# Up projection of a conv-FFN: eight of its 22 column groups computed with tokens on partitions, in chunks of which every second takes seven block products

## The chip, the cores and the metric

The kernel runs on one core of one Trainium2 chip. The time is the device time of one execution in microseconds, here the median of three runs.

## The reference

Two layers on an input of 256 tokens by 2048 features, all in float32. Each layer has a token mixer (a spatial-gating MLP in the first, a latent attention in the second), and then the feed-forward part that this change is about. Cut to that:

```python
D_MODEL, SEQ, D_FF, CONV_W = 2048, 256, 5504, 3

def conv_ffn(x, w_up, conv_w, conv_b, w_down):
    h = x @ w_up                                    # 2048 -> 11008
    h = lax.conv_general_dilated(h, conv_w[:, None, :], window_strides=(1,),
                                 padding=[(CONV_W - 1, 0)], ...,
                                 feature_group_count=C) + conv_b   # causal, per channel
    a, g = jnp.split(h, 2, axis=-1)
    return (jax.nn.silu(g) * a) @ w_down            # 5504 -> 2048

for i in range(2):
    m = gmlp_mixer(x, ...) if i == 0 else mla_mixer(x, ...)
    x = layer_norm(ALPHA * x + m, ...)
    x = layer_norm(ALPHA * x + conv_ffn(x, ...), ...)
```

## The kernel before

**Precision.** Each product of float32 matrices is made of three products of a shorter type: a number is split into a high part and the remainder, and the kernel adds high·high, low·high and high·low. Weights come as chunks of 1 MB (128 partitions by 2048). The class `Feed` loads them (`raw`, three rooms, SyncE's queue), casts the high part `wh` on ScalarE (L125) and subtracts to get the low part `wl` on VectorE (L128). Split chunks live in 14 rooms called "big"; six more are called "side". PSUM has eight banks of 512 columns. Temporaries are in two rings, `t1` (6) and `t2` (5).

**Sevens.** A product of 2×2 blocks needs eight block products; with sums of blocks it needs seven (the Strassen–Winograd form). The kernel uses this for pairs of k: `Feed._seven` makes four sums `ts` of the chunk's blocks on VectorE (L135) and splits both `raw` and `ts`, into `wh`, `wl`, `th`, `tl`; `Banks.seven` issues 21 products of 512 columns, `Banks.eight` 24. A `seven` needs four more banks (`p1`, `q5`, `p7`, `p6`, called OWN) besides the four DIRECT ones (`q3`, `p2`, `e`, `q4`), sums of activation blocks (`combine`), and at the end of a group `rest`, which makes the four corrections from the OWN banks. The first mixer's input projections, its output projection and the down projections work so already. In the first of these, the v projection, a group has eight chunks in the order 0, 2, 1, 3, 5, 4, 6, 7, with sevens at 2, 3, 4 and 6.

**Parked sevens.** Eight chunks of each down projection are prepared during the up projection: `Feed.park` loads one over GpSimd's queue (`praw`), splits it (`pwh`, `pwl`), adds its blocks, splits the sums (`pth`, `ptl`), and stores all four in DRAM; `Feed.fetch` brings them back (`fwh`, `fwl`, `fth`, `ftl`). A unit is four steps of an iterator, advanced by `next(jobs, None)`. Unit 266 is the last parked of the first layer; 231 and 236 are the first two that the down projection uses. These tiles take "side" rooms.

**The up projection** has 86 chunks per layer in 22 groups (four chunks each, the last two). A group is 256 channels of `a` and the same of `g`. Group 0 is computed with tokens on partitions beside the norm of the mixer (`boundary`). Groups 1 to 21 have weights stationary (`prod_a`): per chunk 16 products of 512 columns with `wh`, which multiply high and low parts of the activations at once, and 16 of 256 with `wl`. Their result has channels on partitions, as the convolution along tokens wants it. `sum_halves` adds the two halves (`lo_`, `h_`), `conv` makes bias and three taps (`c_`), `pair` the gate. In groups 2 to 5 the norm's other parts are loaded back and finished (`restore`, `park` of the class `Norm`, on `res` and `lnp`). The first three activations for the down projection are made in groups 19 and 20 (`acts.make`, `dn00wx` and others).

The program's scheduler fixes each engine's order when the kernel is built, under the dependencies and with the rooms available; an instruction then waits on its engine's queue for semaphores, and all behind it wait too.

## Time and profile before

| | |
|---|---|
| median of three runs | 2465.41 us (2465.39 to 2465.87) |
| profiled execution: span | 2464.6 us, and its clock at 1.000 |
| TensorE (PE) busy | 2458.1 us, 100% |
| VectorE (DVE) busy | 2054.7 us, 83% |
| ScalarE (ACT) busy | 1459.3 us, 59% |
| up projection, TensorE, products with `wh`, `wl` | 611.4 us, 328.1 us busy (2624 each) |

The profile is of one execution, on one core, whose span is 0.8 us below the median. A row of the timeline gives start, length, engine, line, operation and, in square brackets, how long the engine had been idle before it and what ended that. A row of a window gives the busy time of PE, PEld (weight load), DVE, ACT and POOL (GpSimd), with the count of instructions, then the clock granted to TensorE, the DMA engines' busy share and GB/s. Lengths overlap where an engine starts the next instruction before the last has drained, so the distance between two starts may be shorter than the first one's length. The chain of waits is the chain of work that ended last.

### The profile page before, as it was taken

What the parts mean: (1) busy time and instruction counts of PE and PEld (TensorE: products, weight loads), DVE (VectorE), ACT (ScalarE), POOL (GpSimd) and SP (SyncE); (2) the same over time, 40 slices, a digit from 0 to 9 for tenths busy, and PEclk for the clock granted to TensorE, in tenths of its full rate; (3) what the DMA queues carried; (4) which work ended last, traced back from release to release, by engine and by line L of the source; (5) the groups of instructions that cost most, each with busy time, mean ns of one, the idle gap of its engine ahead of it and who ended that gap; (6) DMA issues with size and microseconds to landing.
All of it is one profiled execution on the core that took longest, in us unless ns stands there. A gap on an engine that the chain in (4) does not pass through costs nothing. (4 is left out here: it accounts for less than half of the span.)

```text
span 2464.6 us, 32483 instructions
## 1 busy us (share of the span) xinstructions
PE 2458.1 (100%) x12494; PEld 2091.3 (85%) x12494; DVE 2054.7 (83%) x2734; ACT 1459.3 (59%) x1967; POOL 104.2 (4%) x202
## 2 busy tenths in 40 slices
PE   9999999999999999999999999999999999999999
PEld 7888888888888888888888888988888888888887
DVE  7999999989897788778777997867598787878798
ACT  6666665566565666656554566665565665555453
POOL 0000000000000000000001000000000000000000
PEclk9999999999999999999999999999999999999999
DMA  7555666656665778778868885544478787777885
GB/s 291 202 208 205 226 204 202 205 188 205 222 212 198 241 282 314 300 279 300 322 218 318 301 301 182 184 170 156 172 269 309 275 305 304 295 265 278 299 324 201
DMA packets 116428, 611.94 MB, mean 248 GB/s; under 512 B 10648, under 2 KB 10912, under 8 KB 75184
## 3 DMA queue, kind: packets, MB, share of 16 engines
q1 hardware_dynamic: 90128, 462.47, 52.9%
q0 software_dynamic: 26144, 147.39, 15.8%
q8 instruction: 98, 1.61, 0.3%
q14 instruction: 58, 0.48, 0.1%
HBM read 544.75 MB, written 65.06 MB: 247 GB/s over the span
## 5 line engine op out<-in xcount | busy, mean ns | idle before, releaser
L128 DVE TENSOR_TENSOR wl<-raw,wh 128x1024 fp32r<-128x1024 f32 (+4 forms) x645 | 958.4, 1501 | 169.5 <-ACT wh L125 124.0
L125 ACT CAST wh<-raw 128x1024 fp32r<-128x1024 f32 (+4 forms) x645 | 809.0, 1278 | 356.8 <-PE up L230 80.7
L230 PE MATMUL up<-xhl,wh 128*128 128x512 f32 x2624 | 611.4, 390 | 0.0
L230 PEld LDWEIGHTS up<-xhl,wh 128*128 128x128 f32 x2624 | 487.4, 188 | 97.8
L230 PEld LDWEIGHTS up<-xhl,wl 128*128 128x128 f32 x2624 | 325.8, 192 | 6.4
L230 PE MATMUL up<-xhl,wl 128*128 128x256 f32 x2624 | 328.1, 283 | 0.0
L125 ACT CAST th<-ts 128x1536 fp32r<-128x1536 f32 (+1 forms) x138 | 142.5, 1052 | 110.9 <-DVE ts L135 80.3
L230 PE MATMUL ub<-wh,xhl 128*128 128x512 f32 x576 | 179.5, 393 | 0.0
L128 DVE TENSOR_TENSOR tl<-ts,th 128x1536 fp32r<-128x1536 f32 (+1 forms) x138 | 163.2, 1221 | 10.4 <-PE dn_p L230 3.4
L230 PEld LDWEIGHTS ub<-wh,xhl 128*128 128x128 f32 x576 | 108.1, 188 | 24.2 <-issue 1.9
L230 PE MATMUL ub<-wl,xhl 128*128 128x512 f32 x288 | 112.1, 389 | 0.0
L135 DVE TENSOR_TENSOR ts<-ts,raw 128x512 f32<-128x512 f32 x138 | 95.1, 689 | 1.4
L135 DVE TENSOR_TENSOR ts<-raw 128x1024 f32<-128x1024 f32 x69 | 84.3, 1221 | 6.1 <-PE ub L230 3.8
L230 PE MATMUL mo<-wh,oT 128*128 128x512 f32 x256 | 82.5, 401 | 0.0
L230 PE MATMUL v_q<-wh,xhl 128*128 128x512 f32 x224 | 70.7, 391 | 0.3 <-ACT wh L125 0.3
L230 PEld LDWEIGHTS ub<-wl,xhl 128*128 128x128 f32 x288 | 54.1, 188 | 11.3
L230 PE MATMUL v_p<-wh,xhl 128*128 128x512 f32 x192 | 59.9, 389 | 0.0
L230 PEld LDWEIGHTS mo<-wh,oT 128*128 128x128 f32 x256 | 45.5, 189 | 7.1
L230 PEld LDWEIGHTS v_q<-wh,xhl 128*128 128x128 f32 x224 | 42.0, 188 | 10.5 <-ACT wh L125 1.9
L230 PE MATMUL mo<-wl,oT 128*128 128x512 f32 x128 | 50.1, 391 | 0.0
L724 ACT ACTIVATE lny<-lnt,lncol 128x128 f32<-128x128 f32 x96 | 36.6, 472 | 15.6 <-PE lnt L720 15.5
L388 DVE TENSOR_TENSOR h_0a<-up,lo_0a 128x256 f32<-128x256 f32 x41 | 17.2, 421 | 33.0 <-ACT lo_0a L386 33.0
(1838 smaller groups left out, 4338.4 us busy)
## 6 DMA issues: line engine op xcount, KB each, us to landing
raw<-in_ffn_up_dram SPq DMA_DIRECT2D x172, 1024.0 KB, 7.0
raw<-in_gm_in_dram SPq DMA_DIRECT2D x93, 1024.0 KB, 5.3
raw<-in_ffn_dn_dram SPq DMA_DIRECT2D x68, 1024.0 KB, 7.2
raw<-in_gm_wout_dram SPq DMA_DIRECT2D x48, 1024.0 KB, 5.3
praw<-in_ffn_dn_dram POOLq DMA_DIRECT2D x16, 1024.0 KB, 13.9
keptth<-pth POOLq DMA_DIRECT2D x16, 1024.0 KB, 8.1
kepttl<-ptl POOLq DMA_DIRECT2D x16, 1024.0 KB, 8.8
fth<-keptth POOLq DMA_DIRECT2D x16, 1024.0 KB, 9.4
```

The lines of the kernel that those rows point to most:

```text
L125: cast = self.nc.scalar.copy(hi, raw)
L128: self.nc.vector.tensor_tensor(lo, raw, hi.bitcast(F32), ALU.subtract)
L135: add = lambda o, a, b: self.nc.vector.tensor_tensor(o, a, b, ALU.add)
L230: recent[0] = nc.tensor.matmul(o, l, r, start=start, stop=stop, skip_group_check=True)
L388: nc.vector.tensor_tensor(h, acc[:, 0:S], lo, ALU.add)
L724: nc.scalar.activation(y[:, j], t[:, j * P : (j + 1) * P], AF.Identity, bias=lncol[:, o : o + 1], scale=lncol[:, g : g + 1])
```

## The change

Per layer, groups 5 and 6 together, and 8 and 9 together, become one *token group* each: eight chunks with tokens on partitions, each chunk 256 k by 1024 columns, in the v projection's order and with sevens at the same four places. A token group has all eight banks. `sum_acts` makes the four activation sums that sevens need, two in group 2 and two in group 4, in two "side" rooms. After the last chunk `rest` and four more sums give the group's four results in SBUF; in the next group (7 and 10), behind its first chunk, 16 transposes (`turn_group`) bring them to channels on partitions, in four banks `upr`, and behind its second and third chunk the convolutions and gates follow (`gate_group`), reading those banks without `sum_halves`. Parked work leaves groups 5, 6, 8 and 9: its steps now stand in groups 2 to 4, at the end of 7 and 10, and in groups 11 to 20, three in odd and two in even ones. All four norm restores move to groups 1 and 2, the norm's parking to 2 and 3. Line numbers grow: L125, L128, L135 and L230 become L129, L132, L139 and L234.

```diff
--- before.py
+++ after.py
@@ -52,6 +52,10 @@
 U_PAIRS = [[0, 1, 5, 7, 2, 6, 3, 4]] + [[0, 1, 2, 5, 3, 7, 4, 6]] * 5
 U_SEVEN = [(2, 3)] + [(2, 3, 4)] * 4 + [(2, 3)]
 
+UP_TOKEN = (5, 8)
+UP_PAIRS = (0, 2, 1, 3, 5, 4, 6, 7)
+UP_SEVEN = (2, 3, 4, 6)
+
 T1, T2 = 6, 5
 SLOTS = {"big": 14, "raw": 3, "side": 6}
 
@@ -264,14 +268,27 @@
                     parked.append(len(chunks))
                 chunks.append((w[2 * u : 2 * u + 2, :, c].rearrange("k p c -> p k c"), 2048, kind))
 
+    def up(layer):
+
+        for gi in range(22):
+            if gi - 1 in UP_TOKEN:
+                continue
+            if gi not in UP_TOKEN:
+                chunks.extend((ffn_up[layer, i], 2048, "") for i in range(4 * gi, min(4 * gi + 4, n_up)))
+                continue
+            for p in UP_PAIRS:
+                i = 4 * gi + p // 2
+                w = ffn_up[layer, i : i + 5 : 4, :, p % 2 * 1024 : p % 2 * 1024 + 1024].rearrange("f p c -> p f c")
+                chunks.append((w, 2048, "seven" if p in UP_SEVEN else "wide"))
+
     back(gm_wout, NF_GM)
-    chunks += [(ffn_up[0, i], 2048, "") for i in range(n_up)]
+    up(0)
     back(ffn_dn[0], NF_FF)
     chunks += [(ml_q[i], 2048, "") for i in range(4)]
     chunks += [(ml_kv[i], 3 * KVR, "") for i in range(5)] + [(ml_kv[5, :, 0:KVR], KVR, "")]
     chunks += [(ml_b[i], 2048, "") for i in range(ml_b.shape[0])]
     chunks += [(ml_out[i], 2048, "") for i in range(ml_out.shape[0])]
-    chunks += [(ffn_up[1, i], 2048, "") for i in range(n_up)]
+    up(1)
     back(ffn_dn[1], NF_FF)
 
 
@@ -940,26 +957,83 @@
         boundary(ln, acc, end, f"upf{layer}_", after)
         xhl, old = ln.new, ln
         jobs = park_all(feed.used + 2 * n_up)
+        sums, rooms, turning = {}, [], []
+
+        def sum_acts(p):
+
+            if len(sums) % 2 == 0:
+                rooms.append(slot([P, 2, 8 * P], f"xs{layer}_{p}", F32R, "side" if len(rooms) < 2 else "big"))
+            t = xhl[p // 2][:, 2 * (p % 2) : 2 * (p % 2) + 2]
+            raw = tp.tile([P, 2, S], F32, tag="t2", name=f"xr{layer}_{p}", bufs=T2)
+            nc.vector.tensor_tensor(raw, t[:, :, 0:S].bitcast(F32), t[:, :, S : 2 * S].bitcast(F32), ALU.add)
+            sums[p] = combine(f"{layer}_{p}", rooms[-1][:, len(sums) % 2, :], raw[:, 0], raw[:, 1])
+
+        def token_group(gi):
+
+            acc = Banks(f"upt{layer}_{gi}", DIRECT + OWN)
+            for c, p in enumerate(UP_PAIRS):
+                a = [[x_parts(xhl, 2 * p + j, b) for j in range(2)] for b in range(2)]
+                got = feed.next()
+                if p in UP_SEVEN:
+                    acc.seven(a, sums[p], *got, turned=512, across=True)
+                    if p == [q for q in UP_PAIRS if q in UP_SEVEN][-1]:
+                        rest = acc.rest()
+                else:
+                    acc.eight(a, *got, across=True)
+            for n, t in zip(DIRECT, rest):
+                nc.vector.tensor_tensor(t, acc.acc[n], t, ALU.add)
+            turning.append((gi, rest, [bank(f"upr{layer}_{gi}_{i}") for i in range(4)]))
+
+        def turn_group():
+
+            gi, rest, t = turning[0]
+            for i, r in enumerate(rest):
+                b, f = i // 2, i % 2
+                for j in range(4):
+                    o = (j % 2) * S + b * P
+                    nc.tensor.transpose(t[2 * f + j // 2][:, o : o + P], r[:, j * P : (j + 1) * P], ident)
+
+        def gate_group(f):
+
+            gi, rest, t = turning[0]
+            for j in range(2):
+                c = slice(j * S, (j + 1) * S)
+                pair(2 * (gi + f) + j, t[2 * f][:, c], t[2 * f + 1][:, c])
+            if f == 1:
+                turning.pop()
+
         for gi in range(1, 22):
+            if gi - 1 in UP_TOKEN:
+                continue
+            if gi in UP_TOKEN:
+                token_group(gi)
+                continue
             nt, nk = (4, 4) if gi < 21 else (2, 8)
             acc = [bank(f"up{layer}_{gi}_{f}") for f in range(nt)]
             for c in range(KD // nk):
                 hi, lo = feed.next()
                 prod_a(acc, xhl, range(nk * c, nk * c + nk), hi, lo)
-                if gi > 1 and c in (1, 2) and gi + c > 3:
+                if gi > 1 and c in ((1, 2, 3) if gi > 10 and gi % 2 or gi - 2 in UP_TOKEN else (1, 2)) and gi + c > 3 and not turning:
                     next(jobs, None)
                 if (gi, c) in FIRST:
                     acts.make(*plan(NF_FF)[0][FIRST.index((gi, c))])
+                if turning and c == 0:
+                    turn_group()
+                if turning and c in (1, 2):
+                    gate_group(c - 1)
+                if gi in (2, 4) and c < 2 and len(sums) < len(UP_SEVEN):
+                    sum_acts(UP_SEVEN[len(sums)])
                 if gi == 1 and c == 0:
                     after(1, 1, None)
                     for f in range(2):
                         pair(f, hb[0][:, f * S : (f + 1) * S], hb[1][:, f * S : (f + 1) * S])
             for f in range(nt // 2):
                 pair(2 * gi + f, acc[f], acc[nt // 2 + f])
-            if 1 < gi < 6:
-                old.restore(gi - 2)
-            if gi in (4, 6):
-                old.park(gi // 2 - 2)
+            if gi < 3:
+                old.restore(2 * gi - 2)
+                old.restore(2 * gi - 1)
+            if gi in (2, 3):
+                old.park(gi - 2)
         ln = Norm(2 * layer + 1, {}, old.put_away, last)
         return (ln, *down(NF_FF, act, f"dn{layer}", ln, acts, 4 if last else SKEW))
```

Three places of the new order. Names are those of the tiles with their buffer numbers; a chunk's number stands in `wh178` and the like; layer 0 is shown.

TensorE, second token group, in what were groups 8 and 9. Before, the start of group 8, where chunks 176 and 177 follow one another in plain products (the first products with `wh176`, and with `wl177`):

```order
L230 MATMUL up0_8_0_7592<-xhl1_0_5782,wh176_7470 128x512 [waits Activation_49]
L230 MATMUL up0_8_1_7593<-xhl1_0_5782,wh176_7470 128x512 [waits DVE_49,PE_49]
L230 MATMUL up0_8_2_7594<-xhl1_0_5782,wh176_7470 128x512 [waits DVE_49]
L230 MATMUL up0_8_3_7595<-xhl1_0_5782,wh176_7470 128x512 [waits DVE_49,PE_49]
L230 MATMUL up0_8_0_7592<-xhl1_1_5783,wl177_7515 128x256 [waits DVE_49]
L230 MATMUL up0_8_1_7593<-xhl1_1_5783,wl177_7515 128x256
```

Now the same weights' place, chunks 177 and 178:

```order
L234 MATMUL upt0_8_e_7562<-wh178_7568,xhl1_0_5782 128x512 x2
L234 MATMUL upt0_8_e_7562<-wl178_7569,xhl1_0_5782 128x512
L234 MATMUL upt0_8_q4_7563<-wh178_7568,xhl1_0_5782 128x512 x2
L234 MATMUL upt0_8_p7_7566<-th177_7469,xs0_2_6345 128x512 [waits DVE_49]
L234 MATMUL upt0_8_p7_7566<-th177_7469,xs0_2_6345 128x512
L234 MATMUL upt0_8_p7_7566<-tl177_7470,xs0_2_6345 128x512
L234 MATMUL upt0_8_q4_7563<-wl178_7569,xhl1_0_5782 128x512
L234 MATMUL upt0_8_q4_7563<-wh178_7568,xhl1_0_5782 128x512 x2
L234 MATMUL upt0_8_q4_7563<-wl178_7569,xhl1_0_5782 128x512
L234 MATMUL upt0_8_p6_7567<-th177_7469,xs0_2_6345 128x512 [waits DVE_49,PE_49]
```

The products `p7` and `p6` of chunk 177 stand inside chunk 178, and wait for VectorE.

VectorE at the end of group 7. Before, half-sums, convolutions and the gate of group 7's last pair and group 8's first, with the split of chunk 181:

```order
L388 TENSOR_TENSOR h_0g15_7583<-up0_7_3_7381,lo_0g15_7581 128x256 [waits Activation_49]
L910 SCALAR_TENSOR_TENSOR c_0a15_7577<-h_0a15_7575,cst_176,c_0a15_7577 128x254 [waits DVE_49]
L128 TENSOR_TENSOR wl181_7727<-raw181_7642,wh181_7726 128x1024 [waits Activation_49]
L908 SCALAR_TENSOR_TENSOR c_0g15_7585<-h_0g15_7583,cst_176,c_0g15_7585 128x255 [waits Activation_49]
L910 SCALAR_TENSOR_TENSOR c_0g15_7585<-h_0g15_7583,cst_176,c_0g15_7585 128x254 [waits DVE_49]
L925 TENSOR_TENSOR act0_1_6893<-s0_15_7589,c_0a15_7577 128x256 [waits Activation_49]
L388 TENSOR_TENSOR h_0a16_7769<-up0_8_0_7592,lo_0a16_7767 128x256 [waits Activation_49]
L908 SCALAR_TENSOR_TENSOR c_0a16_7771<-h_0a16_7769,cst_176,c_0a16_7771 128x255 [waits Activation_49]
L388 TENSOR_TENSOR h_0g16_7777<-up0_8_2_7594,lo_0g16_7775 128x256 [waits Activation_49]
L910 SCALAR_TENSOR_TENSOR c_0a16_7771<-h_0a16_7769,cst_176,c_0a16_7771 128x254 [waits DVE_49]
L908 SCALAR_TENSOR_TENSOR c_0g16_7779<-h_0g16_7777,cst_176,c_0g16_7779 128x255 [waits Activation_49]
```

Now, the same pair (15) between the sums and splits of chunk 179:

```order
L132 TENSOR_TENSOR wl179_7600<-raw179_7480,wh179_7599 128x1536 [waits PE_49,Activation_49]
L139 TENSOR_TENSOR ts179_7598<-ts179_7598,raw179_7480 128x512 [waits DVE_49]
L942 TENSOR_TENSOR act0_1_6957<-s0_14_7538,c_0a14_7526 128x256 [waits Activation_49]
L405 TENSOR_TENSOR h_0a15_7543<-up0_7_1_7285,lo_0a15_7541 128x256 [waits Activation_49]
L925 SCALAR_TENSOR_TENSOR c_0a15_7545<-h_0a15_7543,cst_176,c_0a15_7545 128x255 [waits Activation_49]
L405 TENSOR_TENSOR h_0g15_7551<-up0_7_3_7287,lo_0g15_7549 128x256 [waits Activation_49]
L927 SCALAR_TENSOR_TENSOR c_0a15_7545<-h_0a15_7543,cst_176,c_0a15_7545 128x254 [waits DVE_49]
L132 TENSOR_TENSOR tl179_7602<-ts179_7598,th179_7601 128x1536 [waits PE_49]
L925 SCALAR_TENSOR_TENSOR c_0g15_7553<-h_0g15_7551,cst_176,c_0g15_7553 128x255 [waits Activation_49]
L132 TENSOR_TENSOR tl179_7602<-ts179_7598,th179_7601 128x512
L927 SCALAR_TENSOR_TENSOR c_0g15_7553<-h_0g15_7551,cst_176,c_0g15_7553 128x254 [waits DVE_49]
L132 TENSOR_TENSOR wl180_7636<-raw180_7572,wh180_7635 128x2048 [waits DMAHW7_49,PE_49,Activation_49]
```

`h_0a15`, which frees a bank of group 7, now stands behind `ts179` and `wl179`.

VectorE at the start of the down projection. Before, the last parked unit was split in group 17 (first fence), and at the down projection's start chunk 233 and pair 42 stood alone (second fence):

```order
L128 TENSOR_TENSOR wl219_9770<-raw219_9653,wh219_9769 128x1024
L167 TENSOR_TENSOR ptl266_9810<-praw266_9430,pth266_9809 128x2048 [waits DMASW1_49,Activation_49]
L908 SCALAR_TENSOR_TENSOR c_0g35_9718<-h_0g35_9716,cst_176,c_0g35_9718 128x255 [waits Activation_49]
L128 TENSOR_TENSOR wl220_9818<-raw220_9735,wh220_9817 128x1024 [waits DMAHW7_49,PE_49,Activation_49]
L910 SCALAR_TENSOR_TENSOR c_0g35_9718<-h_0g35_9716,cst_176,c_0g35_9718 128x254 [waits DVE_49]
L128 TENSOR_TENSOR wl220_9818<-raw220_9735,wh220_9817 128x1024 [waits Activation_49]
```

```order
L135 TENSOR_TENSOR ts233_10504<-ts233_10504,raw233_10401 128x512
L910 SCALAR_TENSOR_TENSOR c_0g42_10447<-h_0g42_10445,cst_176,c_0g42_10447 128x254 [waits DVE_49]
L128 TENSOR_TENSOR tl233_10508<-ts233_10504,th233_10507 128x1536 [waits PE_49,Activation_49]
L925 TENSOR_TENSOR act0_5_10322<-s0_42_10451,c_0a42_10439 128x256 [waits Activation_49]
L128 TENSOR_TENSOR tl233_10508<-ts233_10504,th233_10507 128x512 [waits DVE_49]
L488 TENSOR_TENSOR dn04wx_10549<-act0_1_6893,dn04wx_10549 128x2x256 [waits Activation_49]
```

Now:

```order
L132 TENSOR_TENSOR tl233_10446<-ts233_10442,th233_10445 128x1536 [waits PE_49,Activation_49]
L171 TENSOR_TENSOR ptl266_10213<-praw266_9978,pth266_10212 128x2048 [waits DMASW1_49,DMASW6_49,PE_49,Activation_49]
L505 TENSOR_TENSOR dn00wx_9935<-act0_0_6104,dn00wx_9935 128x2x256
L942 TENSOR_TENSOR act0_5_10260<-s0_40_10277,c_0a40_10265 128x256 [waits DVE_49]
L942 TENSOR_TENSOR act0_5_10260<-s0_41_10296,c_0a41_10284 128x256
L405 TENSOR_TENSOR h_0g42_10383<-up0_21_1_10300,lo_0g42_10381 128x256 [waits DVE_49,Activation_49]
L132 TENSOR_TENSOR tl233_10446<-ts233_10442,th233_10445 128x512 [waits Activation_49]
```

`ptl266` stands between the two halves of `tl233`, ahead of the split of `dn00wx` and of pair 42's half-sum. ScalarE there, now:

```order
L129 CAST th233_10445<-ts233_10442 128x1536 [waits DVE_49,PE_49]
L170 CAST pth266_10212<-praw266_9978 128x2048 [waits DMASW5_49,DMASW0_49,PE_49]
L403 COPY lo_0g42_10381<-up0_21_1_10300 128x256 [waits DVE_49,Activation_49]
L129 CAST th233_10445<-ts233_10442 128x512
L924 ACTIVATE c_0g42_10385<-h_0g42_10383,cst_176 128x256 [waits DVE_49]
L504 CAST dn04wx_10487<-act0_1_6957 128x2x256 [waits DVE_49]
```

`pth266` waits for TensorE to free a "side" room, and `lo_0g42` stands behind it.

## Prediction

> **What bounds the kernel now.** I read in this order: the page's busy times, the clock, the chain of waits, then two stages by window, then VectorE's rows in each of them.
>
> The page's first lines and the core's clock:
>
> ```profile
> span 2464.6 us, 32483 instructions
> PE 2458.1 (100%) x12494; PEld 2091.3 (85%) x12494; DVE 2054.7 (83%) x2734; ACT 1459.3 (59%) x1967; POOL 104.2 (4%) x202
> ```
>
> ```profile
> core 0: 2464.6 us, clock 1.000
> ```
>
> TensorE is busy for all but 6.5 of 2464.6 us at full clock. A change gains only what it takes out of TensorE's row, and loses what it makes TensorE wait. VectorE, at 83%, is the engine to watch. The profiled span lies 0.8 us under the median of the runs, 2465.41; I make the sum against the span and add 0.8.
>
> The chain of waits has the second layer's up projection as one piece:
>
> ```profile
> 1782.32 450.10 PE up L230 x2592
> ```
>
> 2592 products are 81 chunks of 32, so a chunk costs 5.557 us, without one gap. The first mixer's v projection already does what the change does to the up projection: groups of eight chunks, four of them sevens. The copies with which its groups end, TensorE's rows around a block of 16 transposes, and busy times by window (PE, PEld, DVE, ACT, POOL; a v group, a u group, then up groups 2 to 4, 5 and 6, 7 and 8 of the first layer):
>
> ```profile
> L450 ACT COPY v1p<-v_p x1: 589/589/589, 83.9 to 83.9; 128x512 f32<-128x512 f32 x1
> L450 ACT COPY v2p<-v_p x1: 589/589/589, 124.7 to 124.7; 128x512 f32<-128x512 f32 x1
> ```
>
> ```profile
> 455.26 1.91 PE L858 MATMUL ub<-ident,v 128*128 128x128 f32 x16
> 456.92 0.71 PE L230 MATMUL ub<-wh,xc 128*128 128x512 f32 x2
> ```
>
> ```profile
> 84.10:124.90 40.80, 40.80 (x182) 33.78 (x181) 39.61 (x37) 27.39 (x34) 0.00 (x0) 1.00 0.59 207
> 400.00:446.00 46.00, 46.00 (x210) 37.85 (x209) 42.41 (x43) 26.99 (x29) 2.14 (x4) 1.00 0.63 203
> 837.40:904.10 66.70, 66.70 (x386) 59.07 (x385) 57.87 (x88) 36.95 (x55) 3.93 (x7) 1.00 0.89 319
> 904.10:948.50 44.40, 44.40 (x257) 39.34 (x256) 38.20 (x52) 29.41 (x41) 2.87 (x5) 1.00 0.74 277
> 948.50:993.00 44.50, 44.50 (x258) 39.39 (x257) 33.13 (x48) 24.46 (x36) 2.87 (x5) 1.00 0.77 299
> ```
>
> A v group takes 40.80 us with VectorE busy for 39.61 of it, and TensorE does not wait there. In the up stage VectorE has 6 to 11 us of idle time per window; the change spends it.
>
> **The change, part by part.**
>
> *Products.* Four token groups (groups 5+6 and 8+9 in both layers) replace eight chunks each. Removed: 8 × 5.557 = 44.46 us. In their place stand four `eight` of 24 products and four `seven` of 21, which is 180 products of 512 columns. A v group is those 180 and lasts 124.7 − 83.9 = 40.80 us. Gain per token group: 3.66 us.
>
> *Transposes.* 16 of 128×128 turn each token group back. The block above starts at 455.26 and its successor at 456.92: 1.66 us. Same shape and type, so I take 1.66; the bounds are 1.4 (four transposes spent 0.35 us elsewhere, from 1781.72 to 1782.07) and 1.91 (the block's own length).
>
> ```profile
> 1781.72 0.60 PE L938 MATMUL uph<-ident,upt 128*128 128x128 f32 x4
> 1782.07 2.15 PE L230 MATMUL up<-xhl,wl 128*128 128x256 f32 x16
> ```
>
> Net 3.66 − 1.66 = 2.00 us per token group, 8.0 in all (7.0 to 9.0 with those bounds). Without any new wait: 2464.6 − 8.0 + 0.8 = 2457.4 us. Everything else in this text is about waits.
>
> *VectorE's work.* What counts is the step from one start to the next, which is shorter than an instruction's length. VectorE in the v group:
>
> ```profile
> 83.69 2.29 DVE L128 TENSOR_TENSOR wl<-raw,wh 128x2048 fp32r<-128x2048 f32 x1
> 85.89 1.22 DVE L135 TENSOR_TENSOR ts<-raw 128x1024 f32<-128x1024 f32 x1
> 87.02 0.68 DVE L451 TENSOR_TENSOR v1u<-v_p,v1p 128x512 f32<-128x512 f32 x1
> 87.62 0.68 DVE L135 TENSOR_TENSOR ts<-ts,raw 128x512 f32<-128x512 f32 x1
> 88.22 0.68 DVE L452 TENSOR_TENSOR v1w<-v_q,v1u 128x512 f32<-128x512 f32 x1
> ...
> 90.02 1.75 DVE L128 TENSOR_TENSOR wl<-raw,wh 128x1536 fp32r<-128x1536 f32 x1
> 91.69 0.69 DVE L135 TENSOR_TENSOR ts<-ts,raw 128x512 f32<-128x512 f32 x1
> 92.29 1.75 DVE L128 TENSOR_TENSOR tl<-ts,th 128x1536 fp32r<-128x1536 f32 x1
> 93.95 0.69 DVE L788 TENSOR_TENSOR v<-v_q,v1w 128x512 f32<-128x512 f32 x1
> ```
>
> Steps: 2048 columns 2.20 us, 1536 columns 1.67, 1024 columns 1.13, 512 columns 0.60. So a `seven` costs 1.13 + 0.60 + 1.67 + 0.60 + 1.66 + 0.60 = 6.26, a wide chunk 2.20. In the up stage:
>
> ```profile
> 863.20 1.23 DVE L128 TENSOR_TENSOR wl<-raw,wh 128x1024 fp32r<-128x1024 f32 x1 [1.75 <-ACT wh L125]
> 864.35 0.42 DVE L388 TENSOR_TENSOR h_0a<-up,lo_0a 128x256 f32<-128x256 f32 x1
> 864.68 1.21 DVE L128 TENSOR_TENSOR wl<-raw,wh 128x1024 fp32r<-128x1024 f32 x1
> 865.81 1.75 DVE L167 TENSOR_TENSOR pwl<-praw,pwh 128x1536 fp32r<-128x1536 f32 x1
> 867.48 0.48 DVE L908 SCALAR_TENSOR_TENSOR c_0a<-h_0a,cst,c_0a 128x255 f32<-128x255 f32 x1
> 867.88 0.42 DVE L388 TENSOR_TENSOR h_0g<-up,lo_0g 128x256 f32<-128x256 f32 x1
> ```
>
> A plain chunk costs 2 × 1.13 = 2.27, a half-sum 0.33, a convolution step 0.40, the gate product 0.33 (like a half-sum). An ordinary group is 4 × 2.27 + 4 × 0.33 + 8 × 0.40 + 2 × 0.33 = 14.3 us of VectorE in 22.2 of TensorE. A token group is 4 × (6.26 + 2.20) + 8 × 0.60 (four in `rest`, four final sums) = 38.6, plus its convolutions, done in the group behind it without half-sums, 16 × 0.40 + 4 × 0.33 = 7.7: together 46.3, where two ordinary groups had 28.6. So VectorE gets some 18 us more per token group and about 9 more per layer for the four sums of activations: 2 × (2 × 18 + 9) = 90 us in all. The three up windows hold 26 us of idle time in 156, an estimate of 150 over the two stages of 450 us, so the sum fits; what matters is where it falls.
>
> *Where it is tight.* From the start of group 5 to the end of group 10 VectorE has 2 × 46.3 + 2 × 14.3 + two steps of parked work (a step is about a quarter of 1.67 + 4 × 0.60 + 2.20, so 1.6) = 124.4 us. TensorE has 2 × 40.8 + 2 × 22.2 + 2 × 1.66 = 129.4. That is 96%; the v group, by the same steps, is (4 × 8.46 + 8 × 0.60) / 40.8 = 95%, and does not stall. Groups 2 to 4 get 3 × 14.3 + four sums of 2.25 + five steps of parked work of 1.6 + some 8 of restores = 68 us of VectorE in 66.7 of TensorE. That is 1.3 late if it enters them with nothing done ahead, and its idle 8.8 us there in the old order show that it does run ahead, so nothing is taken for it. Walking the new order row by row with these steps, the first token group finds all its parts in time (closest: 2.4 us). In the second, `p7` of chunk 177 must wait for its bank, which the half-sum `h_0a15` of group 7 frees; the walk has that at 79.2 us after the start of group 5, with TensorE there at 78.4. Loss: 0.8 us per layer. The same walk over the old order has the row below at 871.8, 2.4 us early after 33 us, because VectorE also waits for ScalarE (the 1.75 above).
>
> ```profile
> 874.16 0.69 DVE L152 TENSOR_TENSOR praw<-praw 128x512 f32<-128x512 f32 x1
> ```
>  I therefore take 1.1 us per layer, 0.8 from the walk and 0.3 because only waits inside this last stretch add; bounds 0 (ScalarE as early as in the v group) and 3.2 (the walk's whole error on top).
>
> *Start of the down projection.* The eighth parked unit now ends behind group 20 instead of 18, and in the new order its cast `pth266` waits for a room that TensorE frees with chunk 231. Behind it stand, on ScalarE, the lo copies of pair 42, and on VectorE `ptl266` (2.20) and the split of `dn00wx` that chunk 232 multiplies. TensorE fills in with the seventh products of 231; by the order and these steps the split comes just when it is needed, 0 to 0.5 us late. Taken: 0. The stores and fetches of kept weights go through the GpSimd queue, with time to landing, and the old issue times:
>
> ```profile
> keptth<-pth POOLq DMA_DIRECT2D x16, 1024.0 KB, 8.1
> fth<-keptth POOLq DMA_DIRECT2D x16, 1024.0 KB, 9.4
> ```
>
> ```profile
> 1279.43 0.53 POOL L187 DMA_DIRECT2D fwh<-keptwh  x1 [67.33 <-PE dn_p L230]
> 1282.15 0.53 POOL L187 DMA_DIRECT2D fth<-keptth  x1 [1.66 <-PE dn_p L230]
> ```
>
> The fetch of unit 236 now stands on that queue behind the store of `pth266`, about 8 us later than at 1279.43; the first product that needs them comes after chunks 231 to 235, (2 × 21 + 3 × 24) × 0.227 = 25.9 us after chunk 231 starts. The store can start once `pth266` is cast, some 5 us into that time; 8.1 to land, then 9.4 for the fetch make 22.5, and the three fetches behind it come one after the other. Bounds 0 and 7 us per layer (`fth` and `ftl` a whole landing late); taken 0, since `fth` is needed only 9 products after `fwh`, and was issued 2.7 us behind it before.
>
> *At no cost:* the restores and parks of the norm that move to groups 1 to 3 (the old order ran them there already, VectorE's 57.87 of 66.70 holds them); the weights' fetches (same bytes, three raw rooms, the v group pulls 207 GB/s where this stage moved 277 to 319); ScalarE, at 24 to 29 us per 44 in these windows, gets two casts more per `seven`.
>
> Sum: 2464.6 − 8.0 + 2 × 1.1 + 0.8 = 2459.6 us.
>
> **The rivals.** (a) *VectorE becomes the limit for part of the stretch, same within what can be told.* It has 5 us of slack per layer between 124.4 and 129.4. The row below says it waited 124 us in 105 places for ScalarE's casts; the casts of a `seven` alternate with its sums, and the convolutions now read the transposes' banks.
>
> ```profile
> DVE wl L128 <- ACT wh L125: 124.0, 105, 5.2
> ```
>
> If VectorE idles 7 us per layer between groups 5 and 10, TensorE loses 2 to 3; with 0.5 at the down projection and 1 at the restores that makes 2457.4 + 2 × (2.5 + 1) = 2464.4, equal to now.
>
> (b) *Slower: VectorE pays whole lengths, not steps.* By lengths a `seven` is 1.22 + 0.68 + 1.75 + 0.69 + 1.75 + 0.69 = 6.8 and the stretch 138 us against 129.4: 8.7 us late per layer, 2457.4 + 17.4 = 2474.8. Against it: the v group's chunks and sums by lengths are 41.8 us, and it took 40.80. The Trainium skill states this rule ("VectorE: DVE Perf Modes", "The DRAIN you can't avoid": the next instruction does not start until the pipe is empty); the same page weakens it for an instruction that is not held. The trace disagrees with the strict form: 88.22 is 0.60 after 87.62, whose length is 0.68. What remains of this rival is dependence: instructions that wait on the one before pay their length, and waits on ScalarE come on top. It decides from 12 us of lost VectorE time per layer, 5 absorbed and 6.5 passed on: 2470.3.
>
> (c) *Slower at the down projection:* the fetch of unit 236 lands 7 us late in both layers. 2459.6 + 14 = 2473.6. For it: the store ahead of it on the queue; against it: 22.5 us of work in 25.9.
>
> (d) *The clock drops* in the transposes: the 16 in the profile ran at 1.00. I give it nothing.
>
> **How the numbers follow.** Two measurements of this kernel closer than 0.2% (4.9 us) count as the same, so faster means under 2460.5 and slower over 2470.3. My own case, small losses of up to 1.5 us per layer: 2457 to 2460.5, 0.50. Rival (a) 0.36, 2460.5 to 2468. Rivals (b) 0.08 and (c) 0.06, beyond. The range starts at 2456.4 (transposes at 1.4, no wait) and reaches through most of (a) to 2467.5; what lies beyond is (b), (c) and the end of (a). The likeliest case alone is 2456.4 to 2460.5.
>
> **What the new profile would show.** Right: the product groups `upt` with 720 products at 0.227 us per step, four blocks of 16 transposes of 1.66 us, TensorE's busy time down by 8; its idle time before `p7` of the second token group about 1 us, released by VectorE. Wrong: gaps on TensorE ended by `tl` or `wl` inside groups 8 and 9 (rival a or b), by a transfer of `fwh` or `fth` at the start of the down projection (c), or transposes whose block takes more than 1.91 us.

## The result and the profile after

The changed kernel takes 2486.36 us (median of four runs, 2484.85 to 2488.59), the kernel before 2465.40: the ratio is 1.0084, 95% interval 1.0072 to 1.0096. The forecast was 2459.6, and at most 2467.5. Its profiled execution took 2487.55.

The page's first lines and the core's clock, after:

```profile
span 2485.8 us, 32115 instructions
PE 2459.9 (99%) x12254; PEld 2081.2 (84%) x12254; DVE 2137.5 (86%) x2830; ACT 1475.9 (59%) x1947; POOL 104.2 (4%) x202
```

```profile
core 0: 2485.8 us, clock 0.997
```

TensorE is idle for 25.9 us, where it was 6.5; and its busy time has not fallen by 8.0 but risen by 1.8, which goes with a clock of 0.997. TensorE's waits in the up projection, by what released them (total, times, longest):

```profile
PE up L234 <- DVE wl L132: 8.8, 6, 4.3
PE up L234 <- ACT wh L129: 6.6, 2, 4.0
PE upt_q L234 <- DVE wl L132: 2.8, 2, 1.6
```

Only the last row is the token groups' (`upt`). The other two, 15.4 of 18.2 us, are in plain groups. TensorE near the end of the first up projection, groups 19 and 20:

```profile
1244.75 3.82 PE L234 MATMUL up<-xhl,wh 128*128 128x512 f32 x16
1251.14 3.96 PE L234 MATMUL up<-xhl,wh 128*128 128x512 f32 x16 [2.58 <-ACT wh L129]
1255.07 1.22 PE L234 MATMUL up<-xhl,wl 128*128 128x256 f32 x8
1256.60 1.21 PE L234 MATMUL up<-xhl,wl 128*128 128x256 f32 x8 [0.31 <-DVE wl L132]
1262.11 3.78 PE L234 MATMUL up<-xhl,wl 128*128 128x256 f32 x16 [4.29 <-DVE wl L132]
```

TensorE runs out of split weights. After the wait of 4.29 us, 16 products of 256 columns take 3.78 us instead of 2.1: the clock has dropped. ScalarE in the same stretch, and GpSimd's queue:

```profile
1234.75 1.99 ACT L129 CAST wh<-raw 128x1024 fp32r<-128x1024 f32 x2
1248.40 1.47 ACT L170 CAST pwh<-praw 128x1536 fp32r<-128x1536 f32 x1 [11.66 <-DMA praw<-in_ffn_dn_dram]
1249.78 0.36 ACT L403 COPY lo_0a<-up 128x256 f32<-128x256 f32 x1
1250.04 1.99 ACT L129 CAST wh<-raw 128x1024 fp32r<-128x1024 f32 x2
```

```profile
1233.23 0.53 POOL L161 DMA_DIRECT2D kepttl<-ptl  x1 [2.07 <-DVE ptl L171]
1233.80 0.71 POOL L166 DMA_DIRECT2D praw<-in_ffn_dn_dram  x1
```

ScalarE stands still for 11.66 us at the cast of the last parked unit, whose load was issued at 1233.80, only 0.6 us behind the last store of the unit before it. The casts of the up projection's own weights (1250.04) stand behind it on the same queue. Loads of parked units take little longer than before, 15.4 us (median) to landing against 13.9; they are issued later, compared with the cast that needs them. ScalarE's wait for them, before and after:

```profile
ACT pwh L166 <- DMA praw<-in_ffn_dn_dram: 7.9, 3, 6.7
```

```profile
ACT pwh L170 <- DMA praw<-in_ffn_dn_dram: 73.9, 10, 13.1
```

The token groups' own waits are small. At the start of the first one (layer 0), and TensorE around the transposes:

```profile
914.37 0.61 PE L234 MATMUL upt_q<-wh,xhl 128*128 128x512 f32 x2
916.14 0.50 PE L234 MATMUL upt_q<-wl,xhl 128*128 128x512 f32 x1 [1.16 <-DVE wl L132]
```

```profile
952.87 0.60 PE L994 MATMUL upr<-ident,upt_5w 128*128 128x128 f32 x4
...
954.53 2.16 PE L234 MATMUL up<-xhl,wl 128*128 128x256 f32 x16
```

The transposes take 954.53 − 952.87 = 1.66 us, as was taken for them. Windows over groups 2 to 4, the first and the second token group (columns as before: PE, PEld, DVE, ACT, POOL):

```profile
837.40:904.10 66.70, 66.70 (x386) 59.09 (x385) 64.92 (x107) 39.86 (x58) 4.67 (x8) 1.00 0.85 305
905.10:947.33 42.23, 41.07 (x181) 33.21 (x179) 39.09 (x45) 24.83 (x28) 0.00 (x0) 1.00 0.61 210
969.60:1012.00 42.40, 42.40 (x189) 34.87 (x188) 40.38 (x49) 26.09 (x29) 1.09 (x2) 1.00 0.61 214
```

In the second token group, where the forecast had its wait, VectorE is busy for 40.38 of 42.40 us and TensorE never waits.

### The profile page after: what moved, and what is told of

It reads as the page before. It is cut to its first block, busy times and chain, and to the rows that moved or that the text cites. A ratio compares the mean times of both kernels' runs of the same rounds, so it can differ in the third digit from the quotient of the medians.

```text
span 2485.8 us, 32115 instructions
## 1 busy us (share of the span) xinstructions
PE 2459.9 (99%) x12254; PEld 2081.2 (84%) x12254; DVE 2137.5 (86%) x2830; ACT 1475.9 (59%) x1947; POOL 104.2 (4%) x202
## 5 line engine op out<-in xcount | busy, mean ns | idle before, releaser
L132 DVE TENSOR_TENSOR wl<-raw,wh 128x1024 fp32r<-128x1024 f32 (+5 forms) x613 | 942.6, 1555 | 123.7 <-ACT wh L129 92.2
L129 ACT CAST wh<-raw 128x1024 fp32r<-128x1024 f32 (+5 forms) x613 | 795.1, 1323 | 301.2 <-DMA raw<-in_ffn_up_dram 72.8
L234 PE MATMUL up<-xhl,wh 128*128 128x512 f32 x2112 | 498.0, 393 | 6.6 <-ACT wh L129 6.6
L234 PEld LDWEIGHTS up<-xhl,wh 128*128 128x128 f32 x2112 | 395.7, 190 | 87.1 <-ACT wh L129 7.5
L234 PE MATMUL up<-xhl,wl 128*128 128x256 f32 x2112 | 269.4, 285 | 8.8 <-DVE wl L132 8.8
L234 PEld LDWEIGHTS up<-xhl,wl 128*128 128x128 f32 x2112 | 264.8, 193 | 15.8 <-DVE wl L132 10.4
L129 ACT CAST th<-ts 128x1536 fp32r<-128x1536 f32 (+1 forms) x170 | 176.7, 1052 | 137.8 <-DVE ts L139 113.5
L132 DVE TENSOR_TENSOR tl<-ts,th 128x1536 fp32r<-128x1536 f32 (+1 forms) x170 | 200.8, 1217 | 10.3 <-PE dn_p L234 3.4
L234 PE MATMUL ub<-wh,xhl 128*128 128x512 f32 x576 | 179.6, 393 | 0.0
L234 PEld LDWEIGHTS ub<-wh,xhl 128*128 128x128 f32 x576 | 108.2, 188 | 24.2 <-issue 1.9
L139 DVE TENSOR_TENSOR ts<-ts,raw 128x512 f32<-128x512 f32 x170 | 116.5, 685 | 1.8
L139 DVE TENSOR_TENSOR ts<-raw 128x1024 f32<-128x1024 f32 x85 | 103.5, 1218 | 11.1 <-PE ub L234 3.8
L234 PE MATMUL ub<-wl,xhl 128*128 128x512 f32 x288 | 112.2, 390 | 0.0
L234 PE MATMUL mo<-wh,oT 128*128 128x512 f32 x256 | 82.5, 402 | 0.0
L234 PE MATMUL v_q<-wh,xhl 128*128 128x512 f32 x224 | 70.5, 390 | 1.5 <-ACT wh L129 1.5
L170 ACT CAST pwh<-praw 128x1536 fp32r<-128x1536 f32 x16 | 23.6, 1478 | 73.9 <-DMA praw<-in_ffn_dn_dram 73.9
L234 PEld LDWEIGHTS ub<-wl,xhl 128*128 128x128 f32 x288 | 54.1, 188 | 11.2
L234 PE MATMUL v_p<-wh,xhl 128*128 128x512 f32 x192 | 59.9, 389 | 0.0
L171 DVE TENSOR_TENSOR pwl<-praw,pwh 128x1536 fp32r<-128x1536 f32 x16 | 28.0, 1753 | 35.9 <-ACT pwh L170 35.9
L234 PEld LDWEIGHTS mo<-wh,oT 128*128 128x128 f32 x256 | 45.5, 189 | 7.1
L234 PEld LDWEIGHTS v_q<-wh,xhl 128*128 128x128 f32 x224 | 42.0, 188 | 10.7 <-ACT wh L129 2.0
L234 PE MATMUL mo<-wl,oT 128*128 128x512 f32 x128 | 50.2, 392 | 0.0
## 6 DMA issues: line engine op xcount, KB each, us to landing
praw<-in_ffn_dn_dram POOLq DMA_DIRECT2D x16, 1024.0 KB, 15.4
```

What stands on the lines that cost most here:

```text
L129: cast = self.nc.scalar.copy(hi, raw)
L132: self.nc.vector.tensor_tensor(lo, raw, hi.bitcast(F32), ALU.subtract)
L139: add = lambda o, a, b: self.nc.vector.tensor_tensor(o, a, b, ALU.add)
L170: pin(nc.scalar.copy(hi[:, 0:cols], raw[:, o : o + cols]))
L171: pin(nc.vector.tensor_tensor(lo[:, 0:cols], raw[:, o : o + cols], hi[:, 0:cols].bitcast(F32), ALU.subtract))
L234: recent[0] = nc.tensor.matmul(o, l, r, start=start, stop=stop, skip_group_check=True)
```

## The experiments

Most of them give the 32 steps of parked work other chunks. A table of (group, chunk) then stands in place of the condition:

```diff
-                if gi > 1 and c in ((1, 2, 3) if gi > 10 and gi % 2 or gi - 2 in UP_TOKEN else (1, 2)) and gi + c > 3 and not turning:
+                for _ in range(PARK.count((gi, c))):
                     next(jobs, None)
```

### Parked work, or token groups?

**parks_late_alone**: the kernel before, with the changed kernel's steps and no token groups.

```diff
+PARK = [(2, 2), (3, 1), (3, 2), (4, 1), (4, 2), (7, 3), (10, 3), (11, 1), (11, 2), (11, 3), (12, 1), (12, 2),
...
+        (18, 1), (18, 2), (19, 1), (19, 2), (19, 3), (20, 1), (20, 2)]
```

> The kernel before, with no token groups, but with the 32 steps of parked work at the chunks where the changed kernel has them (none in groups 5, 6, 8, 9). Theory P: the same two stalls at the end of each up projection and the clock drops, some 9 us of stall and 3 of slow clock per layer, without any token group: 2480 to 2490. Rival V: VectorE has far less to do here, so no stall: 2465 to 2467.

Measured: 2487.03, ratio 1.0089 (1.0074 to 1.0105). TensorE at the same place:

```profile
1252.89 5.45 PE L232 MATMUL up<-xhl,wh 128*128 128x512 f32 x16 [3.45 <-ACT wh L127]
1258.18 2.06 PE L232 MATMUL up<-xhl,wl 128*128 128x256 f32 x16
1263.85 3.79 PE L232 MATMUL up<-xhl,wl 128*128 128x256 f32 x16 [3.62 <-DVE wl L130]
```

The same waits without a single token group: in the profiled executions they sum to 15.2 us, against 15.4 in the plain groups of the changed kernel, though VectorE is busy for only 2057.6 us here. The place of the parked steps alone costs some 21 us; VectorE's load is not what did it. The changed kernel's own 21 us stand behind a gain of 7 to 8 us from its fewer products, so it loses 28 to 29. What the waits in its token groups (2.8 us) leave of the difference is no larger than the scatter of this run (2485.58 to 2491.25).

**parks_spaced**: the changed kernel, three chunks between every load and its cast, the last unit done in group 19.

```diff
+PARK = [(2, 2), (3, 1), (3, 2), (4, 1), (4, 2), (7, 3), (10, 3), (11, 1), (11, 2), (12, 1), (12, 2), (12, 3),
+        (12, 3), (13, 2), (13, 3), (14, 0), (14, 0), ... (17, 3), (17, 3), (18, 2), (18, 3), (19, 0)]
```

> The changed kernel, with the 32 steps of parked work at other chunks: from group 11 on, each unit's load now stands three chunks (16.7 us of TensorE) ahead of the cast that needs it, where the changed kernel often has one chunk (5.6 us), and the last unit ends in group 19 instead of 20. Theory P (ScalarE's queue is blocked by the cast of a parked unit whose load, 15 us, was issued too late; TensorE starves behind it and its clock falls): the stalls near 1248 and 2219 us and both clock drops vanish, what is left are the two short stalls ahead of the first token group (1.3 and 1.8 us); 2457.4 + 3.1 = 2460.5, between 2459 and 2463, clock 1.000. Rival V (VectorE is behind after the token groups, and the end of the stage is where that comes out): the steps hold the same work and are packed closer, so the time stays at 2480 to 2488.

Measured: 2491.45, ratio 1.0107 (1.0092 to 1.0122). Theory P failed in this form, and rival V's number fits no better. ScalarE's waits in it:

```profile
ACT pwh L172 <- DMA praw<-in_ffn_dn_dram: 59.4, 10, 11.1
ACT pth L172 <- DVE praw L158: 27.1, 11, 4.3
```

The distance in the program is not the distance on the chip. A load is issued only after the last store of the unit before, so a unit is one chain: load 15 us, cast, sums, second cast, store, and only then the next load. In the trace of before, 41 to 51 us lie between one load and the next (1119.12 to 1161.88 for the last). With no parked work in groups 5, 6, 8 and 9, six units have to go through behind group 10. Here they were placed every five chunks (27.8 us), but their loads come 28 to 36 us apart, and ScalarE waits for most of them.

**one_token_group**: parks_spaced with `UP_TOKEN = (8,)`.

> As parks_spaced, but groups 5 and 6 are plain groups again and only groups 8 and 9 are one token group (half of the products' saving, and the four sums of activations still made). The sum gives 2465.4 - 4.0 = 2461.4 if the token group in groups 8 and 9 costs no wait; 2462.5 or more if the second token group was the tight place, as predicted.

Measured: 2489.42, ratio 1.0095 (1.0080 to 1.0111). The number says nothing about the token group, because the steps of parks_spaced cost their 25 us here too. The trace does: no wait in groups 8 and 9.

**parks_spaced_4_free**: parks_spaced with the first unit's second split moved from group 4 to the end of group 7.

> As parks_spaced, and the sums of the first parked unit with their split (2.2 us of VectorE, 1.9 of ScalarE) and the load of the second moved out of group 4 to the end of group 7. Theory: VectorE and ScalarE were late at chunk 163 because of what stands in group 4; without 4.5 us of it the stalls of 1.3 and 1.8 us before the first token group go, 2457.4 to 2458.5. Rival: these stalls come from the chain of casts, half-sums and convolutions at the end of group 4, not from the amount of work; then the time is that of parks_spaced.

Measured: 2488.37, ratio 1.0088 (1.0071 to 1.0105). TensorE's waits at the first token groups fell from 1.6 us in each layer to 0.3 and 0.6, with 0.2 in each second one. The time cannot show this, since the executions lie up to 8 us apart (2485.14 to 2493.16).

### Taking the load out of the chain

**parks_load_ahead**: the load of unit n+1 is issued behind the sums of unit n, ahead of its second split and stores; a unit begins every five chunks, as in parks_spaced, with four chunks between its load and its cast, and the last one ends in group 18.

```diff
+    def park_load(self, i):
+        ap = self.chunks[i][0]
+        raw = self.praws[i] = self.pool.tile([P, 2048], F32, tag="side", name=f"praw{i}", bufs=SLOTS["side"])
+        self.pin(self.nc.gpsimd.dma_start(raw.rearrange("p (k c) -> p k c", k=ap.shape[1]), ap))
...
                 add(r[3], r[3], r[2])
+                if nxt is not None:
+                    self.park_load(nxt)
                 yield
```

> The changed kernel with all eight parked units per layer, but the load of a unit is issued behind the block sums of the unit before it, ahead of that unit's last split and stores, where before it came after them; the steps stand so that four chunks (22 us) lie between a load and its cast, and the last unit ends in group 18. Theory C (a parked unit is one chain: load 15 us, cast and split 3, sums and second split 10 or more, and only then the next load; six units of 34 us or more have to go through some 220 us behind group 10, so ScalarE always comes to the cast too early, wherever the steps are put): with loads taken out of the chain the waits for the load go, and the time is 2457.4 + 3.1 = 2460.5, between 2458 and 2465. Rival D (the loads are late because transfers are slow in this stage, or the scheduler pulls the cast forward again): ScalarE still waits 5 us and more per unit, and the time is above 2475.

Measured: 2468.78, ratio 1.0016 (1.0006 to 1.0025): 18 us of the 21 are back. ScalarE's cast no longer waits at all (idle time before it, last column):

```profile
L175 ACT CAST pwh<-praw 128x1536 fp32r<-128x1536 f32 x16 | 23.7, 1480 | 0.0
```

It is 8 us above the sum, which had 3.1 us of waits in all. The wait at the first token group has grown, to the 3.35 us below and 2.95 in the second layer, and behind the first of them the clock is at 0.50 until 922.6:

```profile
913.10 0.40 PE L241 MATMUL upt_p<-tl,xs 128*128 128x512 f32 x1
916.85 1.22 PE L241 MATMUL upt_p<-th,xs 128*128 128x512 f32 x2 [3.35 <-DVE h_0g L412]
```

**load_ahead_no_token**: the kernel before with the same steps and loads.

> The kernel before, no token groups, with the parked steps at the chunks of parks_load_ahead and the loads issued as there. With parks_late_alone (2487.0) it tells whether the order of load and stores alone decides: theory C gives 2465.4 to 2466; rival D (late steps cost whatever the order of the loads): above 2475.

Measured: 2465.49, ratio 1.0001 (0.9991 to 1.0010). With parks_late_alone at 2487.03 this shows theory C: with nothing in groups 5, 6, 8 and 9 either way, the late steps cost 21 us, and with loads taken out of the chain (and the steps placed for it) nothing.

**six_parked** and its control **six_parked_before**: six parked units instead of eight, spaced as before, in the changed kernel and in the kernel before.

```diff
-                "21e 20e 19p 18e 17s 16e 15p 14e 13s 12e 11p 10s 9e 8s 7p 6e 5s 4e 3e 2e 1e 0e")}
+                "21e 20e 19e 18e 17s 16e 15p 14e 13s 12e 11p 10s 9e 8s 7e 6e 5s 4e 3e 2e 1e 0e")}
```

> The changed kernel with six parked units per layer instead of eight (two units of the second half of the down projection are computed with eight block products, 3 products of 0.227 us more each, 2.7 us in all), the last four spaced as in the kernel before, eight chunks each. Theory C: no wait for loads at the end of the stage; 2457.4 + 3.1 + 2.7 = 2463.2, between 2461 and 2466. Rival V (VectorE too full behind the token groups): above 2470.

> The kernel before with six parked units per layer: what two parked units fewer cost by themselves. 4 x 3 x 0.227 = 2.7 us more products and no wait: 2468.1, between 2467 and 2469.

Measured: 2465.62 (1.0001, 0.9991 to 1.0010) and 2468.29 (1.0012, 1.0002 to 1.0021). The control came out at + 2.7 us, as summed. Against it the token groups gain 2.7 us instead of 8.0. The trace of six_parked has 3.9 us of waits at the first token groups, and the clock at 0.50 for 6.8 us at the last of them. **six_parked_4_free**, with group 4 free of parked work:

> As six_parked, with the parked work of group 4 moved to the end of group 7. The short stalls ahead of the first token group (1.3 and 1.8 us) shrink by half as in parks_spaced_4_free: 1.6 us under six_parked, 2461.6, between 2460 and 2465.

Measured: 2463.46 (0.9991, 0.9982 to 1.0001), 2.2 us under six_parked.

### The wait at the first token group

**load_ahead_groups_7_10**: `UP_TOKEN = (7, 10)`, two plain groups between the activations' sums and the first token group.

> As parks_load_ahead (eight parked units, loads taken out of the chain), but the token groups are groups 7+8 and 10+11, so that two plain groups, 5 and 6, lie between the sums of activations (groups 2 and 4) and the first token group; no parked steps in group 4, the first three units' steps in 2, 3, 5 and 6. Theory B (the wait at the start of the first token group is VectorE's backlog from groups 2 to 4, 68 us of work in 66.7, which delays the half-sum that frees a bank): no wait is left, 2457.4 to 2458.5, clock 1.000. Rival H (the wait belongs to the handing over of banks from any plain group to a token group): 3 to 7 us of waits stay at the new place, 2460 to 2465.

Measured: 2470.67 (1.0022, 1.0013 to 1.0031). The wait moved along, which speaks against theory B, though five parked steps stood in groups 5 and 6 here (the first row below is from one of them). VectorE at the start of that token group, and TensorE:

```profile
946.77 2.29 DVE L176 TENSOR_TENSOR ptl<-praw,pth 128x2048 fp32r<-128x2048 f32 x1
...
953.12 2.35 DVE L134 TENSOR_TENSOR tl<-ts,th 128x1536 fp32r<-128x1536 f32 x2
955.39 0.42 DVE L412 TENSOR_TENSOR h_0a<-up,lo_0a 128x256 f32<-128x256 f32 x1
...
964.44 0.42 DVE L412 TENSOR_TENSOR h_0a<-up,lo_0a 128x256 f32<-128x256 f32 x1
```

```profile
961.89 0.39 PE L241 MATMUL upt_p<-wh,xhl 128*128 128x512 f32 x1
964.91 0.73 PE L241 MATMUL upt_p<-th,xs 128*128 128x512 f32 x2 [2.63 <-DVE h_0a L412]
```

TensorE began the token group at 948.95. The half-sums of group 6, which free four of the eight banks, run at 955 to 966, because the first two sevens' sums and splits stand ahead of them and between them. The token group wants all eight banks from its second chunk on.

**load_ahead_2_4_free**: token groups 5 and 8, no parked step from group 4 to 9, all four sums in groups 2 and 3.

```diff
-                if gi in (2, 4) and c < 2 and len(sums) < len(UP_SEVEN):
+                if gi in (2, 3) and c < 2 and len(sums) < len(UP_SEVEN):
```

> As parks_load_ahead (token groups 5+6 and 8+9), but no parked step beside groups 4 to 9 (the first unit's sums and second split stand in group 10) and all four sums of activations in groups 2 and 3. Theory B (backlog of VectorE ahead of the token groups delays the half-sums that free their banks): some 9 us of VectorE work less in groups 3 to 7 takes the wait at the first token group from 3.5 to under 1 us and leaves at most 0.5 at the second: 2457.4 + 2 x 1 = 2459.5, between 2458 and 2462. Theory H (handing over of banks: the half-sums queue behind the first seven's sums and splits whatever came before): 1.5 to 2 us stay at the first token group of each layer, 2461 to 2463.

Measured: 2471.19 (1.0018, 1.0009 to 1.0027). Both expectations were too low. TensorE still waits 3.36 us at the first token group (2.87 in the second layer), as long as in parks_load_ahead. The work ahead of that group is less by four block sums of a parked unit (2.4 us by the steps), and two sums of activations (4.5 us) stand a group earlier. VectorE even stood idle in group 4, so B is out:

```profile
893.24 0.48 DVE L935 SCALAR_TENSOR_TENSOR c_0g<-h_0g,cst,c_0g 128x255 f32<-128x255 f32 x1 [4.74 <-ACT c_0g L934]
```

**wide_first**: the same with two wide chunks at the head of each token group.

```diff
-UP_PAIRS = (0, 2, 1, 3, 5, 4, 6, 7)
+UP_PAIRS = (0, 1, 2, 3, 5, 4, 6, 7)
```

> As load_ahead_2_4_free, with the first two chunks of each token group both computed with eight products (order 0, 1, 2, 3, 5, 4, 6, 7), so that the four extra banks are first needed 5.4 us later and one seven less stands ahead of the half-sums. Theory H: the waits for half-sums go, 2457.4 to 2458.5. Theory B: little change against load_ahead_2_4_free; the two sevens in a row (12.5 us of VectorE against 9.5 of TensorE) may cost 1 to 3 us instead.

Measured: 2463.62 (0.9990, 0.9982 to 0.9999). The waits for half-sums are gone from the trace; 0.3 us are left, at a seven's `wl`. This one edit took 7.6 us off, so the handing over of banks is shown as the second cause. What was left over stood at a new place, one parked unit's second cast, which waited for its block sums, and TensorE behind it:

```profile
1083.09 1.91 ACT L175 CAST pth<-praw 128x2048 fp32r<-128x2048 f32 x1 [4.57 <-DVE praw L164]
```

```profile
1092.88 1.43 PE L241 MATMUL up<-xhl,wh 128*128 128x512 f32 x5 [2.13 <-ACT wh L131]
```

**wide_first_sums_early**: two chunks instead of one between a unit's sums and that cast.

```diff
-PARK = [(2, 2), (3, 1), (10, 0), (10, 3), (11, 0), (11, 1), (11, 2), ...
+PARK = [(2, 2), (3, 1), (10, 0), (10, 2), (11, 0), (11, 1), (11, 3), ...
```

> As wide_first, with two chunks instead of one between a parked unit's block sums and its second cast. In wide_first ScalarE waited 4.6 us at that cast once per layer and TensorE 2.3 and 1.4 us behind it. Without these 3.7 us: 2463.6 - 3.7 = 2459.9, between 2458 and 2462; that is the 8.0 us of the products' sum less 1 to 2 of small waits. If the waits only move to the next unit, 2462 to 2464.

Measured: 2459.49 (0.9975, 0.9965 to 0.9985), the fastest of all, 6.0 us under the kernel before and 27 under the changed one. Its page:

```profile
span 2457.5 us, 32104 instructions
PE 2450.7 (100%) x12254; PEld 2076.3 (84%) x12254; DVE 2137.9 (87%) x2830; ACT 1477.8 (60%) x1947; POOL 104.4 (4%) x202
```

TensorE's busy time is 7.4 us below that of before. The sum of the products, 8.0, was there.

### A third token group

**three_token_groups** (load_ahead_groups_7_10 with groups 13+14 as well, six parked units) and **three_wide_first** (wide_first_sums_early with 11+12 as well, six parked units):

> As load_ahead_groups_7_10 with a third token group per layer (13+14) and six parked units, whose steps then stand in groups 2 to 6, 9, 12 and 15 to 18. Products: two more token groups give 2 x 2.0 us, two parked units fewer cost 1.36 per layer: 2457.4 - 4.0 + 2.7 = 2456.1 without any wait, up to 2460 if VectorE (96% from group 7 to 15) is late somewhere.

> As wide_first_sums_early with three token groups per layer (5+6, 8+9, 11+12) and six parked units. 2459.9 - 4.0 for two more token groups + 2.7 for the parked units taken out = 2458.6, between 2457 and 2462; if a third token group in a row leaves VectorE behind, above 2462.

Measured: 2472.18 (1.0028, 1.0017 to 1.0039) and 2463.04 (0.9990, 0.9981 to 0.9999). The first has the waits of load_ahead_groups_7_10. The second missed its 2458.6 by 4.4 us. VectorE has little room left in its third token group, from 1034.5 on:

```profile
1034.50:1078.00 43.50, 42.58 (x184) 33.85 (x183) 41.94 (x51) 26.94 (x32) 0.00 (x0) 1.00 0.59 213
```

VectorE is busy for 41.94 of 43.50 us, and TensorE waits there for `tl` (0.24 us) and `wl` (0.60). With the same in the second layer and 0.90 us for a half-sum at 1126.31, the waits for VectorE sum to 2.6 us; where the rest of the 4.4 went is not shown. Of the two numbers of token groups that were run, two per layer is the faster.

## Why the prediction was wrong

**The step that failed is the one on VectorE's work "where it is tight": it took the parked work that moves as so many microseconds of VectorE ("two steps of parked work", 1.6 us each) and nothing more.** It priced neither the load with which each unit begins nor where that load then stands on GpSimd's queue, though the page had its 13.9 us to landing. The prediction looked at the parked work's last store and fetch, where the order shows a new wait, and not at its loads, where order shows none: a load that stands three or one chunk ahead of its cast reads alike in it. The rows of before had the measure: 15 to 25 us from issue to cast, with ScalarE waiting in only three of 16 cases. Measured: late steps alone + 21 us, with loads taken out of the chain none.

**The clock** was given nothing, as rival (d) and for the transposes alone. It was not the transposes that made it fall, but the waits. Against wide_first_sums_early, with the same 12254 matrix products and transposes at clock 1.000, TensorE in the changed kernel is idle for 19.1 us more and busy for 9.2 us longer (2459.9 against 2450.7).

**Right by its own working:** the products and transposes (8.0 summed, 7.4 less busy time in wide_first_sums_early; 1.66 us per block, as taken). The steps between VectorE's starts: with 96% by that working, the second token group had no wait, so rival (b), whole lengths, is out, and of rival (a) there is no gap in groups 8 and 9; VectorE's 90 us more show as 2137.5 − 2054.7 = 83. The start of the down projection: some 0.2 us late in both layers, within the 0 to 0.5, and no wait for the fetch, so rival (c) is out.

**Right in kind, wrong in place and size:** a bank freed late by a half-sum, for which `p7` waits. The forecast had it at the second token group with 0.8 us. The changed kernel has it at neither; its 1.2 and 1.6 us at the first one are for `wl` (row 916.14). They are of the size of the 1.3 us by which VectorE would leave groups 2 to 4 late and for which the prediction took nothing; without the parked steps of group 4 they were gone (parks_spaced_4_free), and only waits for half-sums were left. Once the loads no longer held things up, the half-sums were the next thing to be late, and they were at the first token group, with up to 3.4 us. The walk over the order counted steps of VectorE against a start that it took as free; it is the handing over from a plain group that costs, wherever it lies.

That 2459.49 is so close to the forecast of 2459.6 is the time of another kernel: four more edits stand between the change and its sum.

## What to carry to other kernels

When background work is squeezed into fewer places, price its whole chain from load to store, and compare that with the time it now has; a load that waits for a store of the piece before cannot be hidden by moving the piece's other steps. One instruction that waits for a transfer on an engine that also feeds the bottleneck blocks that feed, however small its share of the engine. Where a group that uses all banks follows one that needs its banks read out, let it begin with work that needs only the free ones.

## What the runs showed of the hardware

After a long wait TensorE's clock falls to half for some microseconds. In the changed kernel, the windows around the wait of 4.29 us that ends at 1262.11 (clock in the third column from the end):

```profile
1257.00:1262.00 5.00, 0.81 (x7) 0.60 (x6) 4.96 (x13) 4.35 (x8) 0.53 (x1) 0.84 1.07 417
1262.00:1265.00 3.00, 2.89 (x13) 2.90 (x14) 3.00 (x7) 0.93 (x2) 0.00 (x0) 0.50 1.03 415
1265.00:1268.00 3.00, 3.00 (x13) 2.54 (x11) 2.93 (x4) 3.00 (x4) 0.00 (x0) 0.64 1.05 421
```

The wait of 2.58 us at 1251.14 left it at 1.00. In load_ahead_groups_7_10 two waits of equal length ended differently, 2.63 us in the first layer (until 964.91) and 2.60 in the second (until 1927.12):

```profile
960.55:963.97 3.42, 1.73 (x8) 1.11 (x6) 3.42 (x5) 2.52 (x4) 0.00 (x0) 1.00 0.74 277
963.97:967.38 3.41, 2.47 (x11) 2.03 (x12) 2.46 (x7) 2.08 (x4) 0.00 (x0) 1.00 0.59 163
1923.11:1926.52 3.41, 1.41 (x7) 0.82 (x5) 3.41 (x6) 2.25 (x5) 0.00 (x0) 1.00 0.60 228
1926.52:1929.94 3.42, 2.82 (x7) 2.24 (x8) 2.24 (x6) 1.98 (x4) 0.00 (x0) 0.50 0.68 183
```

The borders of these windows are those of the clock: in all the traces here it changes only at the ends of stretches of 3.41 us that follow one another without a break. The first wait is cut in two by such an end (TensorE busy for 1.73 and 2.47 us of the two stretches), the second lies mostly in one stretch (busy for 1.41 us). Leaving out the start and the end of the program, 18 stretches in these traces began at full clock and had TensorE busy for under 45%; half clock followed all of them. It followed 5 of 21 with 45 to 59%, and none with more. So a wait of about 2.6 us may or may not be followed by half clock for 3.4 or 6.8 us, and a median over runs moves with it: the kernels with such waits scatter by 3 to 8 us, the kernel before by 0.5 to 3. The Trainium skill ("TensorE: Matmul & The Clock Gate", "Part 1: The HAM clock gate (the "warmup" mystery)") has the clock halved after an idle window of about 3.4 us that runs freely, so that the point depends on where in the window one lands. The traces agree with the halving, the 3.4 us and the free run; TensorE need not be idle for all of it, since waits of 2.38 and 0.32 us set it off in the changed kernel (until 2236.27), and in parks_spaced two of 0.72 and 1.04 us (until 1168.03).
